# One layer of a hybrid diffusion backbone: where the weights' squares and scales are taken

## The chip, the cores and the metric

The kernel runs on one core of a Trainium2 chip. Time is that of one launch on the device, in microseconds (us), as the median of three runs. Engines are named as the profile names them: PE (TensorE, matmuls; PEld are its weight loads), DVE (VectorE), ACT (ScalarE), POOL (GpSimd) and SP, whose queue issues the DMAs. Every engine runs its own instructions in the order in which they were written into its program.

## The reference, cut to what matters

One layer: RMS norm of tokens with a scale and shift from a conditioning vector, one input projection `w_in`, latent attention beside a pooled branch, gates, an output projection.

```python
mod = jax.nn.silu(c) @ w_mod[l] + b_mod[l]
shift, scale, gate = jnp.split(mod, 3, axis=-1)
h = _rms(x, norm_g[l]) * (1.0 + scale[:, None, :]) + shift[:, None, :]
u = h @ w_in[l]                                   # 2048 tokens, 1024 -> 1984 columns
uc = hc @ w_in[l]                                 # 256 context tokens, own scale and shift
attn = _attend(q, k_all, v_all)                   # q, k, v from columns 0:448 of u
y = _branches(u, attn, w_pool[l], pool_scale[l]) @ w_out[l]
x_new = x + gate[:, None, :] * y
```

Columns 0:448 of `u` feed attention (the "token" columns). Columns 448:1984 are the "features": for each of four groups a pooled input, its gate and the attention gate, 128 columns each, so 12 feature tiles.

## The kernel before, in words

**Precision.** Every product is taken as three matmuls of a high and a low part (hi·hi, hi·lo, lo·hi). In the startup and in block 0 both sides are float32r; from block 1 on they are float16. A float16 weight tile must first be brought to a common range: the sum of its squares is taken, `scl` is its inverse root, the tile is multiplied by `scl` while it is split, and the result is multiplied by `unscl` as it leaves PSUM.

**Stages.** The startup (the list `STARTUP`) loads the modulation weights, makes the scale and shift columns `ac` and `shc`, loads the four token weight tiles (`load_wtok`), and computes the token columns of the first 512 tokens. Then four blocks of 512 tokens run (`feat(b)`, b = 0 to 3), each with 12 feature tiles of two halves of 256 tokens (24 matmuls each half, in `feat_mm`), 96 steps in all. A table `plan` hangs other work on step numbers: token tiles (`tok`, at `TOK_STEPS`), the production of normalised and transposed half blocks hT (`prod`, at `PROD_AT`; the second half of a block is made at the block's start), the float16 token weights (`tok_weights`, at `TW_AT`), the gate row (`gate_row`). From step 88 attention is mixed in, and the output projection ends the kernel. The order in which instructions stand on each engine is made by a scheduler that goes by this program order, by buffers and by its own estimate of times.

**Feature weights.** `load_w(n)` is called from `feat_mm(n - 2)`; tiles 0 to 11 belong to block 0, 12 to 23 to block 1, and from 24 on the finished float16 tiles come back from the DRAM tensor `wd`. In block 0 a loaded tile `raw` is split at once (ACT line 100, DVE line 101). In block 1 `load_w` only loads the same columns again and squares them (line 248, ACT), and `split_w16`, one tile later, goes through a chain: a matmul with ones over one column (`scale_of`, line 227), a sum and a multiply-add on DVE (229, 230), a power on POOL (231), `unscl` on DVE (234, 235), hi on ACT (238), lo on DVE (239), the store to `wd` (257). So the tile for `feat_mm(n)` is split at `feat_mm(n - 1)`.

**Buffers.** `raw` tiles are of tag M (6 buffers), the split tiles, the half blocks and the loaded `x` of tag B (8). PSUM: 5 banks "A", 2 banks "X" (transposes and scale matmuls share them), 1 bank "O". Loads and stores of these stages all go through SP's one queue.

Of the kernel before, what the change touches and what calls it, by code (L numbers as in the profile page):

```python
# [8 lines left out]
F32 = mybir.dt.float32  # L9
F32R = mybir.dt.float32r  # L10
F16 = mybir.dt.float16
AF = mybir.ActivationFunctionType
ALU = mybir.AluOpType
# [3 lines left out]
KT = D // 128  # L17
# [28 lines left out]
X_AT = {0: "c", 11: 2}  # L46
PROD_AT = {"c": (6, 2), 2: (16, 1), 4: (35, 3), 6: (54, 1)}
GATE_AT = (25, 3)
TW_AT = (5, 2)
KV_AT = 79  # L50
Q_AT = 87
ATT_AT = 88
# [15 lines left out]
def tile_hybrid_block(ctx: ExitStack, tc: tile.TileContext, x, c, cx, c_ctx, w_mod, b_mod, norm_g,  # L68
                      w_in, q_lora_g, w_uq, kv_lora_g, w_ukv, q_norm_g, k_norm_g, w_pool,
                      pool_scale, w_out, rope_t, edge_t, out):  # L70
    nc = tc.nc
    x, cx, out = x[0], cx[0], out[0]
# [4 lines left out]
    cst = ctx.enter_context(tc.tile_pool(name="cst", bufs=1))  # L77
# [7 lines left out]
    def nm(s):  # L85
        uid[0] += 1
        return f"{s}{uid[0]}"

    def st(tag, shape, dt=F32):
        return sb.tile([128] + list(shape), dt, tag=tag, bufs=BUFS[tag], name=nm(tag))  # L90

    def pt(tag, shape=(512,), dt=F32):
        return ps.tile([128, *shape], dt, tag=tag, bufs=PBUFS[tag], name=nm("p" + tag))

    def small(n, tag):
        return sm.tile([128, n], F32, tag=tag, name=nm(tag))

    def split(src, hi, lo, eng=None):

        a = nc.scalar.activation(out=hi, in_=src, func=AF.Copy)  # L100
        (eng or nc.vector).tensor_tensor(out=lo, in0=src, in1=hi if hi.dtype == F16 else hi.bitcast(F32),
                                         op=ALU.subtract)
        return a.ins
# [19 lines left out]
    wd = dr.tile([12, 128, 2, KT, 128], F16, name="wd")  # L123
# [6 lines left out]
    nhalf = cst.tile([128, 8], F32, name="nhalf")  # L130
# [4 lines left out]
    ones2 = cst.tile([128, 128], F32, name="ones2")  # L135
# [3 lines left out]
    ssw = cst.tile([128, 20], F32, name="ssw")  # L139
    scl = cst.tile([128, 16], F32, name="scl")  # L140
    unscl = cst.tile([128, 14], F32, name="unscl")
# [9 lines left out]
    def load(out, in_):  # L151

        d = nc.sync.dma_start(out=out, in_=in_)
        if queue:
            if queue[-1] is not None:
                order(queue[-1], d.ins, "order of the first loads")
            queue.append(d.ins)
# [39 lines left out]
    FORDER = [(f, g) for g in range(H) for f in (G_PIN, G_P, G_A)]  # L197
    wq = []

    wraw16 = []  # L200

    def load_w(n):


        if n >= 24:
            w = st("B", [2, KT, 128], F16)
            nc.sync.dma_start(out=w, in_=wd[n % 12])
            wq.append(w)
            return
        f, g = FORDER[n % 12]  # L210
        raw = st("M", [KT, 128])
        load(out=raw, in_=w_in[:, f + g * 128:f + (g + 1) * 128].rearrange("(k p) n -> p k n", p=128))
        if n >= 12:
            square(raw, n % 12)
            wraw16.append((n % 12, raw))
            return
        w = st("B", [2, KT, 128], F32R)
        split(raw, w[:, 0], w[:, 1])
        wq.append(w)


# [2 lines left out]
    def scale_of(c, cols, bound=1.0):  # L224

        p = pt("X")
        nc.tensor.matmul(p[:, 0:cols.stop - cols.start], lhsT=ones2, rhs=ssw[:, cols], start=True, stop=True)
        t = small(1, "sca")
        nc.vector.reduce_sum(t, p[:, 0:cols.stop - cols.start], axis=AX.X)
        nc.vector.tensor_scalar(out=t, in0=t, scalar1=bound * 2.0 ** -30, scalar2=1e-30, op0=ALU.mult, op1=ALU.add)  # L230
        nc.gpsimd.tensor_tensor(out=scl[:, c:c + 1], in0=t, in1=nhalf[:, 0:1], op=ALU.pow)

    def unscale(c, a, b):
        nc.vector.tensor_tensor(out=unscl[:, c:c + 1], in0=scl[:, a:a + 1], in1=scl[:, b:b + 1], op=ALU.mult)
        nc.vector.reciprocal(out=unscl[:, c:c + 1], in_=unscl[:, c:c + 1])

    def split16(src, hi, lo, scale):
        nc.scalar.activation(out=hi, in_=src, func=AF.Copy, scale=scale)  # L238
        nc.vector.scalar_tensor_tensor(out=lo, in0=src, scalar=scale, in1=hi, op0=ALU.mult, op1=ALU.subtract)

    def square(src, c, scale=1.0):
        n = 1
        for k in src.shape[1:]:
            n *= k
        o = junk[:, 0:n]
        if len(src.shape) == 3:
            o = o.rearrange("p (a b) -> p a b", a=src.shape[1])
        nc.scalar.activation(out=o, in_=src, func=AF.Square, scale=scale, accum_out=ssw[:, c:c + 1])

    def split_w16():  # L250

        n, raw = wraw16.pop()
        scale_of(n, slice(n, n + 1))
        unscale(n, n, 13)
        w = st("B", [2, KT, 128], F16)
        split16(raw, w[:, 0], w[:, 1], scl[:, n:n + 1])
        nc.sync.dma_start(out=wd[n], in_=w)
        wq.append(w)

    def mod_scale(si):  # L260
        for i, v in enumerate((ac, shc)):
            square(v[:, :, si], 16 + 2 * si + i, (32.0, 1.0)[i])
        scale_of(13 + si, slice(16 + 2 * si, 18 + 2 * si), 2.0)
        for o, v in ((acs, ac), (shs, shc)):
            nc.vector.tensor_scalar(out=o[:, :, si], in0=v[:, :, si], scalar1=scl[:, 13 + si:14 + si], scalar2=None,
                                    op0=ALU.mult)
# [2 lines left out]

    def tok_weights():  # L270

        scale_of(12, slice(12, 16))
        for si in range(2):
            unscale(12 + si, 12, 13 + si)
        w = st("W", [2, KT, NTOK], F16)
        wt16.append(w)
        for kk in range(4):
            yield
            raw = st("M", [2, NTOK])
            load(out=raw, in_=w_in[kk * 256:(kk + 1) * 256, 0:NTOK].rearrange("(k p) n -> p k n", p=128))  # L280
            k = slice(2 * kk, 2 * kk + 2)
            split16(raw, w[:, 0, k], w[:, 1, k], scl[:, 12:13])

    wth = [st("B", [2304], F32R) for _ in range(2)]
# [6 lines left out]
    def load_wtok(kk):  # L291
        raw = st("M", [2, NTOK])
        load(out=raw, in_=w_in[kk * 256:(kk + 1) * 256, 0:NTOK].rearrange("(k p) n -> p k n", p=128))
        k0 = kk % 2 * 2
        split(raw, wtok[0][kk // 2][:, k0:k0 + 2, :], wtok[1][kk // 2][:, k0:k0 + 2, :],
              nc.gpsimd if kk in WLO_POOL else None)
        square(raw, 12 + kk)

# [373 lines left out]
    nc.vector.memset(gpc, 0.0)  # L674

    def feat_mm(n, halves, got):
        if wraw16:
            split_w16()
        if n + 2 < 48:
            load_w(n + 2)  # L680
        w = wq.pop(0)
        p = pt("A")
        for i, hf in enumerate(halves):
            hi, lo = hT[hf]
            m = 0
            for kt in range(KT):
                for a, b in ((0, hi), (0, lo), (1, hi)):
                    nc.tensor.matmul(p[:, i * HB:(i + 1) * HB], lhsT=w[:, a, kt, :], rhs=b[:, kt, :],  # L688
                                     start=(m == 0), stop=(m == 23))
                    m += 1  # L690
            if i == 0:
                yield
        got.append(p)
# [66 lines left out]
    def gate_row():  # L760
        acc = st("M", [D])
        for k in range(KT):
            yield
            wr = st("M", [D])
            nc.sync.dma_start(out=wr, in_=w_mod[k * 128:(k + 1) * 128, 2 * D:3 * D])
            if k == 0:
                nc.vector.tensor_scalar(out=acc, in0=wr, scalar1=sc[:, 0:1], scalar2=None, op0=ALU.mult)
            else:
                nc.vector.scalar_tensor_tensor(out=acc, in0=wr, scalar=sc[:, k:k + 1], in1=acc,
                                               op0=ALU.mult, op1=ALU.add)  # L770
        yield
        g = st("M", [D])
        bm = st("M", [D])
        nc.sync.dma_start(out=bm[0:1, :], in_=b_mod[2 * D:3 * D].unsqueeze(0))
        for n in range(2):
            p = pt("X")
            nc.tensor.matmul(p[0:1, :], lhsT=ones, rhs=acc[:, n * 512:(n + 1) * 512], start=True, stop=True)
            nc.vector.tensor_tensor(out=g[0:1, n * 512:(n + 1) * 512], in0=p[0:1, :],
                                    in1=bm[0:1, n * 512:(n + 1) * 512], op=ALU.add)
        nc.sync.dma_start(out=gated.unsqueeze(0), in_=g[0:1, :])  # L780

    def iter_call(f, *a):
        f(*a)
        yield
# [7 lines left out]
    plan = {}  # L792
# [6 lines left out]
    for hf, (s0, d) in PROD_AT.items():  # L799
        g = prod(hf)  # L800
        for i in range(4):
            plan.setdefault(s0 + d * i, []).append(g)
    mod_scale(0)
    plan.setdefault(5, []).append(iter_call(mod_scale, 1))
    g = ctx_cols()
    for i in range(5):
        plan.setdefault(i, []).append(g)
    g = tok_weights()
    for i in range(5):
        plan.setdefault(TW_AT[0] + TW_AT[1] * i, []).append(g)  # L810
    g = gate_row()
    for i in range(10):
# [416 lines left out]

    queue.clear()  # L1230
    load_w(1)
    at = attn()
    step = 0
# [109 lines left out]
```

## Time and profile before

| | |
|---|---|
| Time, three runs | median 1253.59 us (1249.56 to 1254.69) |
| Profiled execution, its own time | 1253.44 us |
| Its span, first to last instruction | 1251.6 us |
| Mean granted clock of PE | 0.978 of full |
| DMA | 216.83 MB |

The profiled execution is one more run. Its time beyond the span, 1.84 us, is launch and end. Granted clock 1.0 is 2.4 GHz, 0.5 is 1.2 GHz. The stages stand in the trace like this: the startup until about 60 us, block 0 until 182, block 1 until 310, blocks 2 and 3 with the first scores of attention from there, attention and the output projection from about 450 on.

### The profile page before, as it was taken

The page shows a single profiled execution, that of the slowest core. Times are in us where ns is not written, and L with a number is a line of the kernel's source. Part 1 is how long each engine was busy: PE and PEld are TensorE (multiplying, and loading weights), DVE is VectorE, ACT ScalarE, POOL GpSimd, SP SyncE. Part 2 cuts the span into 40 slices and gives each one's busy share as a digit, 9 for nine tenths or more (in the row PEclk, how much of TensorE's full clock was granted, in tenths as well). Part 3 has the DMA queues.
Part 4 walks back from the last instruction along what each step waited for, and adds up shares of the span by engine and source line. Part 5 has one row for each costly group of instructions (what it writes and reads, how often), then busy time and mean ns, then how long its engine had stood idle before and what let it go on. Part 6 is the DMA issues. An engine that isn't in the chain of part 4 may idle for free.

```text
span 1251.6 us, 22592 instructions
## 1 busy us (share of the span) xinstructions
PE 1178.1 (94%) x7739; PEld 876.3 (70%) x7739; DVE 900.9 (72%) x1749; ACT 767.3 (61%) x1860; POOL 601.2 (48%) x681
## 2 busy tenths in 40 slices
PE   6899988979999999899999999999999999799998
PEld 2699876857778879665666666666666666688887
DVE  4876765565546445469888787878788866999886
ACT  5585676655666455257777777777777766743221
POOL 3655413432435424013656556555655565226666
PEclk9799999979999999999999999999999999999999
DMA  9437755386535556747978788878978788616532
GB/s 305 148 110 183 191 134 180 111 202 201 175 94 140 139 150 147 192 93 161 230 191 197 169 228 193 192 182 205 222 188 190 192 224 193 195 54 207 193 129 99
DMA packets 192586, 216.83 MB, mean 173 GB/s; under 512 B 92707, under 2 KB 145236, under 8 KB 192342
## 3 DMA queue, kind: packets, MB, share of 16 engines
q1 hardware_dynamic: 192470, 215.38, 65.4%
q8 instruction: 61, 1.00, 0.3%
q14 instruction: 55, 0.45, 0.1%
HBM read 100.33 MB, written 41.85 MB: 114 GB/s over the span
## 4 chain that ended last, share of the span: by engine, by line
PE 75%; ACT 6%; DMA 6%; DVE 6%; issue 3%; POOL 2%; SPq 2%; ACTq 0%; DVEq 0%; POOLq 0%
PE pA L882 20%; PE pA L688 17%; PE pA L1156 12%; PE pO L931 6%; PE pA L338 5%; PE pX L931 5%; PE pX L882 2%; PE pA L617 2%; ACT M L964 2%; ACT T L903 2%; DMA M<-in_w_in_dram 1%; SPq L921 1%; DMA B<-in_w_mod_dram 1%; PE pA L592 1%; DMA W<-W 1%
## 5 line engine op out<-in xcount | busy, mean ns | idle before, releaser
L968 POOL TENSOR_TENSOR M<-W,M 128x512 f16<-128x512 f32 x244 | 277.7, 1159 | 254.5 <-ACT M L964 221.0
L882 PE MATMUL pA<-B,M 128*128 128x512 f16 x1280 | 300.6, 380 | 12.3 <-ACT T L903 8.7
L882 PEld LDWEIGHTS <-M 128*128 128x128 f16 x1600 | 156.4, 98 | 153.6 <-issue 14.5
L906 DVE STREAM_TRANSPOSE W<-T 128x512 f32<-128x512 f32 x310 | 192.9, 641 | 72.3 <-ACT T L903 58.2
L964 ACT ACTIVATE M<-W 128x512 f16<-128x512 f32 x279 | 164.6, 632 | 112.6 <-PE pX L931 43.7
L688 PE MATMUL pA<-B,B 128*128 128x256 f16 x1728 | 212.8, 278 | 12.2 <-ACT B L238 4.9
L931 PEld LDWEIGHTS <-B 128*128 128x128 f16 x1728 | 168.5, 98 | 59.1 <-issue 22.3
L688 PEld LDWEIGHTS <-B 128*128 128x128 f16 x1728 | 169.6, 100 | 43.8 <-issue 6.9
L903 ACT ACTIVATE T<-pA,nm,gm 128x512 f32<-128x512 f32 x248 | 188.9, 770 | 16.2 <-DVE nm L891 16.1
L885 DVE TENSOR_REDUCE mx<-pA 128x1 f32<-128x512 f32 x256 | 169.5, 672 | 16.0 <-PE pA L882 15.5
L1156 PE MATMUL pA<-W,M 128*128 128x512 f32 (+1 forms) x528 | 121.0, 388 | 2.3 <-DVE M L1162 2.3
L931 PE MATMUL pO<-M,B 128*128 128x256 f16 x864 | 114.8, 273 | 8.4 <-POOL M L968 3.7
L931 PE MATMUL pX<-M,B 128*128 128x256 f16 x864 | 112.3, 274 | 5.5 <-DVE M L968 2.9
L1156 PEld LDWEIGHTS pA<-W,M 128*128 128x128 f32 x528 | 98.6, 190 | 22.8 <-DVE M L1162 2.7
L688 PE MATMUL pA<-W,B 128*128 128x256 f32 x576 | 78.5, 288 | 0.0
L688 PEld LDWEIGHTS pA<-W,B 128*128 128x128 f32 x576 | 72.8, 192 | 0.3
L1148 POOL TENSOR_TENSOR B<-T,B 128x512 f32<-128x512 f32 x31 | 50.3, 1625 | 29.6 <-DVE T L1183 27.7
L338 PE MATMUL pA<-W,B 128*128 128x448 f16 (+1 forms) x336 | 63.6, 337 | 0.0
L1148 POOL TENSOR_TENSOR T<-T,M 128x512 f32<-128x512 f32 x27 | 43.1, 1596 | 38.4 <-DVE T L1197 27.6
L1161 ACT ACTIVATE M<-B 128x512 fp32r<-128x512 f32 x32 | 19.7, 628 | 51.6 <-PE pA L1156 39.1
L903 ACT ACTIVATION_READ_ACCUMULATOR T<-pA,nm,gm 128x1 f32 x248 | 48.8, 197 | 0.0
L338 PEld LDWEIGHTS <-B 128*128 128x128 f16 x336 | 31.8, 98 | 22.4 <-issue 0.2
(246 smaller groups left out, 1848.2 us busy)
## 6 DMA issues: line engine op xcount, KB each, us to landing
W<-W SPq DMA_DIRECT2D x496, 144.0 KB
M<-in_w_in_dram SPq DMA_DIRECT2D x24, 512.0 KB
B<-wd SPq DMA_DIRECT2D x24, 512.0 KB
B<-in_x_dram SPq DMA_DIRECT2D x16, 512.0 KB
B<-brd SPq DMA_DIRECT2D x8, 1024.0 KB
B<-in_x_dram SPq DMA_DIRECT2D x8, 1024.0 KB
out_dram<-B SPq DMA_DIRECT2D x31, 256.0 KB
wd<-B SPq DMA_DIRECT2D x12, 512.0 KB
```

What stands on the lines that cost most here:

```text
L338: nc.tensor.matmul(p[:, c0:NTOK], lhsT=a[:, kt, k * 128:(k + 1) * 128], rhs=b, start=(kt == 0 and n == 0), stop=(kt == KT - 1 and n == 2))
L617: nc.tensor.matmul(qp[:, 0:384], lhsT=a[:, i, :], rhs=uq[w][:, i, b * 384:(b + 1) * 384], start=(n == 0), stop=(n == 5))
L688: nc.tensor.matmul(p[:, i * HB:(i + 1) * HB], lhsT=w[:, a, kt, :], rhs=b[:, kt, :], start=(m == 0), stop=(m == 23))
L882: nc.tensor.matmul(b[:, s0:s0 + sn], lhsT=q[:, a, c, p % 2, i], rhs=kt[ki][:, kc, o:o + sn], start=(m == 0), stop=(m == 4))
L885: nc.vector.reduce_max(mx[:, n:n + 1], b[:, :w], axis=AX.X)
L903: nc.scalar.activation(out=e[:, :w], in_=sp[n][:, :w], func=AF.Exp, bias=ng, scale=escale, accum_out=rs[:, n:n + 1])
L906: nc.vector.transpose(TP[p][:, :, i, j0:j1, :].rearrange("p q j b -> p j q b"), e[:, :w].rearrange("p (j q b) -> p j q b", q=4, b=32))
L931: i = nc.tensor.matmul(o, lhsT=V[0][:, j, a], rhs=t[:, c, jj], start=(j == 0 and m == 0), stop=(j == NJ - 1 and m == 2))
L964: a = nc.scalar.activation(out=t[:, 0], in_=s2, func=AF.Copy)
L968: lo = eng.tensor_tensor(out=t[:, 1], in0=s2, in1=t[:, 0], op=ALU.subtract)
L1148: eng.tensor_tensor(out=o[:, c0:c1] if op == ALU.mult else xr[:, k, n, c0:c1], in0=o[:, c0:c1], in1=a[:, c0:c1], op=op)
L1156: nc.tensor.matmul(b[:, c0:c1], lhsT=c[:, x0, kt, :], rhs=w[x1][:, kt, c0:c1], start=(first and kt == kts[0] and m == 0), stop=(last_ and ...
```

## The change

The squares of the feature tiles move from block 1 to block 0, where each tile is loaded for the first time; `feature_scales` makes all twelve scales at once, at `feat_mm(10)`. In block 1 `load_w(n)` then splits the tile where it loads it, one tile earlier in the program than before. The squares of the token weights leave the startup: `tok_weights` takes them from the hi halves `wth` at step 3 (with a bound of 2 in the scale) and goes on at steps 5 to 13, as before. `mod_scale(0)` moves from ahead of step 0 to step 2.

```diff
-TW_AT = (5, 2)
+TW_AT = (3, 2)
     def load_w(n):
         if n >= 12:
-            square(raw, n % 12)
-            wraw16.append((n % 12, raw))
-            return
-        w = st("B", [2, KT, 128], F32R)
-        split(raw, w[:, 0], w[:, 1])
+            w = st("B", [2, KT, 128], F16)
+            split16(raw, w[:, 0], w[:, 1], scl[:, n - 12:n - 11])
+            nc.sync.dma_start(out=wd[n - 12], in_=w)
+        else:
+            w = st("B", [2, KT, 128], F32R)
+            split(raw, w[:, 0], w[:, 1])
+            square(raw, n)
         wq.append(w)
-    def split_w16():
-
-        n, raw = wraw16.pop()
-        scale_of(n, slice(n, n + 1))
-        unscale(n, n, 13)
-        w = st("B", [2, KT, 128], F16)
-        split16(raw, w[:, 0], w[:, 1], scl[:, n:n + 1])
-        nc.sync.dma_start(out=wd[n], in_=w)
-        wq.append(w)
+    def feature_scales():
+
+        p = pt("X")
+        nc.tensor.matmul(p[:, 0:12], lhsT=ones2, rhs=ssw[:, 0:12], start=True, stop=True)
+        t = cst.tile([128, 12], F32, name="fsc")
+        nc.vector.tensor_scalar(out=t, in0=p[:, 0:12], scalar1=2.0 ** -30, scalar2=1e-30, op0=ALU.mult, op1=ALU.add)
+        nc.gpsimd.tensor_tensor(out=scl[:, 0:12], in0=t, in1=nhalf[:, 0:1].broadcast_to([128, 12]), op=ALU.pow)
+        nc.vector.tensor_scalar(out=unscl[:, 0:12], in0=scl[:, 0:12], scalar1=scl[:, 13:14], scalar2=None, op0=ALU.mult)
+        nc.vector.reciprocal(out=unscl[:, 0:12], in_=unscl[:, 0:12])
     def tok_weights():
-        scale_of(12, slice(12, 16))
+        for i in range(4):
+            square(wth[i // 2][:, i % 2 * 896:i % 2 * 896 + 896].bitcast(F32), 12 + i)
+        yield
+        scale_of(12, slice(12, 16), 2.0)
     def load_wtok(kk):
-        square(raw, 12 + kk)
     def feat_mm(n, halves, got):
-        if wraw16:
-            split_w16()
+        if n == 10:
+            feature_scales()
-    mod_scale(0)
+    plan.setdefault(2, []).append(iter_call(mod_scale, 0))
     g = tok_weights()
-    for i in range(5):
+    for i in range(6):
```

Lines of the changed kernel below are a few higher for the same code (548 was 546, 327 was 325, 559 was 557, 646 was 644).

ACT at the start of block 0, before: T are token results leaving PSUM (line 546) and being squared (557), B_630, B_637 and B_792 are the feature tiles 1 to 3, M their raw tiles.

```order
L100 ACTIVATE W_115<-T_529 128x512
L546 COPY T_610<-pA_240 128x448
L100 ACTIVATE B_630<-M_628 128x1024
L557 ACTIVATE junk,us_669<-T_610 128x256
L557 ACTIVATE junk,us_669<-T_610 128x128
L546 COPY T_612<-pA_247 128x448
L557 ACTIVATE junk,us_669<-T_610 128x64
L100 ACTIVATE B_637<-M_635 128x1024
L100 ACTIVATE B_792<-M_790 128x1024
```

The same place after the change (B_617, B_625 and B_781 are tiles 1 to 3).

```order
L100 ACTIVATE W_115<-T_526 128x512
L100 ACTIVATE B_617<-M_615 128x1024
L248 ACTIVATE junk,ssw<-M_615 128x1024
L100 ACTIVATE B_625<-M_623 128x1024
L248 ACTIVATE junk,ssw<-M_623 128x1024
L548 COPY T_607<-pA_239 128x448
L100 ACTIVATE B_781<-M_779 128x1024
L548 COPY T_609<-pA_246 128x448
L559 ACTIVATE junk,us_658<-T_607 128x256
L559 ACTIVATE junk,us_658<-T_607 128x128
L559 ACTIVATE junk,us_658<-T_607 128x64
```

The first token result now stands behind two splits and two squares; before it stood ahead of all of them.

ACT at the change from block 0 to block 1, before: B_2154 is the float16 feature tile 12, the first of block 1; pX_2101 and pA_2190 belong to token tiles, pA_2161 is the result of feature tile 11.

```order
L738 ACTIVATE T_2065<-pA_2070 128x512
L100 ACTIVATE B_1856<-T_2060 128x512
L642 ACTIVATE T_2106<-pX_2101,gqk 128x512
L599 ACTIVATE junk,sk_2194<-pA_2190 128x128
L586 ACTIVATE T_2186<-T_1968 128x128
L599 ACTIVATE junk,sk_2194<-pA_2190 128x128 x3
L238 ACTIVATE B_2154<-M_2067,scl 128x1024
L744 ACTIVATE T_2235<-pA_2161 128x512
```

The same place after (B_2088 is tile 12, B_2170 tile 13).

```order
L327 ACTIVATE T_2072<-pX_2067,shs,acs 128x256 x2
L238 ACTIVATE B_2088<-M_2086,scl 128x1024
L100 ACTIVATE T_2119<-pX_2117 128x128
L740 ACTIVATE T_2077<-pA_2092 128x512
L238 ACTIVATE B_2170<-M_2168,scl 128x1024
L100 ACTIVATE B_1867<-T_2072 128x512
L644 ACTIVATE T_2128<-pX_2123,gqk 128x512
```

Tile 12 moved ahead of the token tile's work and of the gate's result, and tile 13, which before came some ten rows later, now stands close behind it.

SP's queue at the same place, before: B_2245 is the half block of `x` that `prod(3)` turns into hT for the second half of block 1; kd and vd are stores of keys and values; M_2546 is the raw tile 16.

```order
L153 DMA M_2546<-in_w_in_dram 128x8x128
L589 DMA vd<-T_1980 128x256
L644 DMA kd<-T_2106 128x4x128
L652 DMA kd<-U_2117 128x4x128
L645 DMA kd<-T_2107 128x4x128
L589 DMA vd<-T_2186 128x256
L153 DMA B_2245<-in_x_dram 128x1024 x2
L745 DMA gad<-T_2235 128x512
L756 DMA brd<-T_2242 128x504
L257 DMA wd<-B_2154 128x2048
```

And after (B_2258 is that half block of `x`, B_2088 and B_2170 the tiles 12 and 13, M_2529 the raw tile 16).

```order
L591 DMA vd<-T_1992 128x256
L153 DMA M_2529<-in_w_in_dram 128x8x128
L153 DMA B_2258<-in_x_dram 128x1024 x2
L214 DMA wd<-B_2088 128x2048
L767 DMA M_2560<-in_w_mod_dram 128x1024
L646 DMA kd<-T_2128 128x4x128
L214 DMA wd<-B_2170 128x2048
L647 DMA kd<-T_2129 128x4x128
L591 DMA vd<-T_2199 128x256
```

The load of `x` moved ahead of the three stores of keys that stood before it. In both programs SP has 465 rows; no DMA is added or removed.

## Rows read from the trace of the kernel before

**Rows 1.** The page, part 1: busy time of each engine, its share of the span, instructions.
```profile
...
PE 1178.1 (94%) x7739; PEld 876.3 (70%) x7739; DVE 900.9 (72%) x1749; ACT 767.3 (61%) x1860; POOL 601.2 (48%) x681
...
```

**Rows 2.** Windows: length, busy time and count by engine, granted clock, DMA.
```profile
...
60.00:182.00 122.00, 116.88 (x891) 112.06 (x890) 84.09 (x186) 82.74 (x232) 52.44 (x88) 0.97 0.59 152
182.00:310.00 128.00, 110.31 (x807) 87.19 (x808) 75.38 (x168) 76.70 (x188) 43.94 (x84) 0.92 0.60 172
310.00:450.00 140.00, 139.59 (x1070) 112.80 (x1068) 72.67 (x155) 83.88 (x256) 57.38 (x116) 1.00 0.54 142
450.00:1252.00 802.00, 767.33 (x4816) 538.44 (x4814) 628.41 (x1172) 488.66 (x1126) 415.04 (x365) 0.99 0.69 178
...
```

**Rows 3.** PE's waits, 182 to 310: in total, times, longest.
```profile
...
PE pA L688 <- ACT B L238: 4.9, 3, 3.2
PE pA L688 <- DVE B L239: 4.7, 2, 2.3
PE pX L227 <- DVE U L651: 2.1, 2, 1.8
PE pX L657 <- DVE U L651: 2.1, 1, 2.1
PE pA L688 <- DVE B L101: 1.4, 3, 0.5
PE pX L320 <- ACT T L325: 1.0, 2, 0.8
...
```

**Rows 4.** Timeline of PE: start, duration, instruction, idle before it and what ended it.
```profile
...
58.50 1.11 PE L338 MATMUL pA<-B,W 128*128 128x448 f32 x2 [1.26 <-DVE W L101]
...
188.36 4.87 PE L688 MATMUL pA<-B,B 128*128 128x256 f16 x22 [2.32 <-DVE B L239]
...
223.06 0.28 PE L227 MATMUL pX<-ssw,ones 128*128 128x1 f32 x2
223.20 2.78 PE L688 MATMUL pA<-B,B 128*128 128x256 f16 x24
...
261.78 4.36 PE L688 MATMUL pA<-B,B 128*128 128x256 f16 x24
...
276.03 5.30 PE L688 MATMUL pA<-B,B 128*128 128x256 f16 x24 [2.34 <-DVE B L239]
...
```

**Rows 5.** Timeline of ACT, at four places.
```profile
...
69.96 0.54 ACT L546 COPY T<-pA 128x448 f32<-128x448 f32 x1 [1.36 <-PE pA L338]
...
72.87 1.05 ACT L100 ACTIVATE B<-M 128x1024 fp32r<-128x1024 f32 x1
...
122.96 1.06 ACT L100 ACTIVATE B<-M 128x1024 fp32r<-128x1024 f32 x1 [2.44 <-DMA M<-in_w_in_dram]
...
184.45 1.15 ACT L238 ACTIVATE B<-M,scl 128x1024 f16<-128x1024 f32 x1 [0.97 <-POOL scl L231]
...
```

**Rows 6.** Line 239, VectorE's half of the split: shortest, median, longest ns.
```profile
...
L239 DVE SCALAR_TENSOR_TENSOR B<-M,scl,B x12: 1256/1278/1286, 187.0 to 306.3; 128x1024 f16<-128x1024 f32 x12
...
```

**Rows 7.** Line 111, powers on POOL, one column and four.
```profile
...
L111 POOL TENSOR_TENSOR kvr<-kvm,nhalf x18: 542/576/911, 73.7 to 471.5; 128x1 f32<-128x1 f32 x18
L111 POOL TENSOR_TENSOR kr<-km,nhalf x18: 1012/1018/1029, 85.9 to 489.1; 128x4 f32<-128x4 f32 x18
...
```

**Rows 8.** Timeline of SP's queue around the load of the fourth half block.
```profile
...
181.63 0.37 SPq L644 DMA_DIRECT2D kd<-T  x1
...
184.16 0.87 SPq L153 DMA_DIRECT2D B<-in_x_dram  x2
...
```

**Rows 9.** Line 248, the squares: one instruction and its read of the sum.
```profile
...
L248 ACT ACTIVATE junk<-M x16: 933/1056/1098, 15.3 to 289.1; 128x1024 bf16<-128x1024 f32 x12, 128x896 bf16<-128x896 f32 x4
L248 ACT ACTIVATION_READ_ACCUMULATOR junk<-M x16: 185/187/243, 16.1 to 290.1; 128x1 f32 x16
...
```

**Rows 10.** PE's waits, 60 to 182.
```profile
...
PE pO L751 <- ACT T L100: 3.2, 1, 3.2
PE pA L592 <- ACT T L100: 1.5, 1, 1.5
```

More of the change, by code (lines that the diff above doesn't have):

```diff
@@ L198, in tile_hybrid_block @@
     wq = []
-    wraw16 = []
     def load_w(n):
```

## Prediction

> **What bounds the kernel now.** I read the page's first part, then the windows by stage, then PE's waits in the stages where PE is not full, and last the timelines around those waits. PE is busy 94% of the span, and no other engine comes near it [rows 1], so time is won where PE stands idle or runs at the half clock, and lost where the change makes it stand. The windows say where that is [rows 2]: block 0 (60 to 182) has 122.00 - 116.88 = 5.1 us without PE work, block 1 (182 to 310) has 128.00 - 110.31 = 17.7 us and a mean granted clock of 0.92, and from 310 to 450 PE is busy 139.59 of 140.00 us at clock 1.00. What block 1 is shortened by is therefore not taken back by a wait in the stage behind it, as far as the order of the instructions there stays the same, which it does past block 2 but for a few swaps of neighbours.
>
> What PE waits for in block 1 [rows 3]: 4.9 us for line 238 and 4.7 us for line 239, the two halves of the split that close the chain of a feature tile, and 2.1 us at line 227, the chain's own matmul, which waits for a bank "X" that a token tile still holds (`U` of line 651). Another 2.1 us go to a transpose waiting for the same tile, 1.4 and 1.0 us to the hT of the next half block. ACT's row at 184.45 shows the chain from its other side: the split has waited 0.97 us for the power of line 231 [rows 5].
>
> The clock: 24 matmuls of a half take 2.78 us at full clock. After 2.32 us of idle time 22 of them take 4.87, after 2.34 us 24 take 5.30, and between them stands one half of 4.36 [rows 4]; these are the rows that answer to a granted clock of 1.2 GHz in place of 2.4. Against the undisturbed half that is 4.87 - 22/24 x 2.78 = 2.3, 5.30 - 2.78 = 2.5 and 4.36 - 2.78 = 1.6, in all 6.4 us.
>
> **The change, part by part.** The sum is made against the profiled execution's 1253.4 us, which stands 0.15 us below the median of the three runs.
>
> *The chain leaves block 1.* Twelve chains go, and the tile is split one tile earlier, a time in which PE has about 2 x 2.78 = 5.6 us of matmuls to do. The split itself needs 1.15 on ACT and 1.28 on DVE, one after the other, 2.4 us [rows 5, 6], so it fits under one tile unless the raw tile or a buffer is late. I take all of 4.9 + 4.7 + 2.1 = 11.7 us as gone. Three things come in their place. First, one chain remains, at the border of the blocks: matmul, DVE, POOL, ACT, DVE. The power over 12 columns has no row; one column takes 0.55, four take 1.02 [rows 7], and a line through both gives 0.39 + 12 x 0.157 = 2.3 us; the bounds are 1.0 (no more than four columns) and 12 x 0.55 = 6.6. I take 2.3, since two rows give it. With the split's 2.4 the chain is 4.7 and some 0.5 for the small operation on DVE. PE has behind the chain's matmul 16 matmuls of tile 11 (16 x 0.116 = 1.9 us) and some small token work of about as many columns as 12 such matmuls (an estimate, 1.4 us): 3.3 us. That leaves 1.9. Second, ACT now has tile 13's split ahead of the copy that finishes the hT of the first half of block 1; I count 0.4 for that, bounded by zero and the split's 1.15. Third, the bank "X" for which line 227 waited is still wanted by the next transpose: 1.0 of the 2.1 us stays. Against that stands the load of `x` for the second half of block 1. In before it was issued at 184.16, behind a store of keys issued at 181.63 [rows 8]; it now stands ahead of the stores, and of the 2.4 us of hT waits (1.4 + 1.0, [rows 3]) I take 1.0 as won. Net: -11.7 + 1.9 + 0.4 + 1.0 - 1.0 = -9.4 us. Bounds: nothing left of any wait in the block, -17.7; or the power at 6.6 and both `X` waits whole, -4.
>
> *The clock in block 1.* With the two longest gaps gone their halves run at full clock. One gap of about 2.3 us is left at the border, so I take back 5.0 of the 6.4 us (bounds 2.3, if each border wait again costs a half, and 6.4).
>
> *The matmuls of the chain.* 15 scale matmuls become 4, eleven fewer, each 0.14 us from its start to the start of the next [rows 4]: -1.5 us, since PE is what the stage runs on.
>
> *The startup.* Four squares of about 1.0 us leave ACT [rows 9]. The last wait of PE there is on DVE (line 101, 1.26 us, [rows 4]), whose work for the tiles stays, so most of this is hidden: -0.5, between 0 and -1.3. The modulation columns' squares only move to step 2, where nobody waits for them for the next steps: 0.
>
> *Block 0 pays.* ACT gets 12 squares of feature tiles (1.06 and 0.19 for the read of the sum, [rows 9]) and 4 of token weights; two of the twelve lay in this window before. That is 10 x 1.25 + 4 x 1.05 = 16.7 us, and ACT goes from 82.74 to 99.4 of 122 us, 81%, below PE's 116.88 [rows 2]. On average it is not the bound; the cost is in order. At the start the first token result, which left PSUM at 69.96, stands after the change behind two splits and two squares, the first of which began at 72.87 [rows 5]: its turn comes at about 72.87 + 1.05 + 1.25 = 75.2, 5.2 us later. In PE's order about one half of a feature tile is put ahead of the work that needs it, some 2.6 us, so 2.6 are uncovered. Later in the block a square can stand ahead of a result for which PE waits; I put 1.4 on that, a bit more than one square. Total +4. Bounds: nothing (the squares run in ACT's gaps), or all of the 16.7 and more.
>
> Here a row speaks against the change. At 122.96 ACT's split waited 2.44 us for a raw tile [rows 5], and in the same block PE waited 3.2 us at line 751 and 1.5 at line 592 for ACT's line 100 [rows 10]: whatever ACT is made to hold, what stands behind it is held as well. The Trainium skill, "Perfetto Trace Analysis", section "Tensor Engine Instruction (MATMUL, LD_WEIGHTS)", says that ACT, DVE and GPSIMD take their work strictly first in, first out, and only PE can reorder a little. The trace agrees, with those 2.44 and 3.2 us. By that rule each of the twelve squares is a delay of 1.25 us for all results behind it on ACT, and if PE waited for each of them, the time would be the one of the third rival below.
>
> **Sum.** -9.4 - 5.0 - 1.5 - 0.5 + 4.0 = -12.4, and 1253.4 - 12.4 = 1241.0 us.
>
> **The rivals.**
>
> *The wait only changes its name.* The splits of block 1 come earlier by a tile, but so must the raw tiles; if the load, a buffer of tag M or B, or a bank "X" is what comes last next, half of the 11.7 us stays and with it half of the clock: -12.4 + 5.9 + 2.5 = -4.0, or 1249; with a little luck at the buffers 1246. For it speaks that the 2.1 us at line 657 are already such a wait [rows 3]; against it, that the longest waits name lines 238 and 239 and not a DMA.
>
> *Block 0 eats the gain.* ACT at 81% delays results often enough that block 0 becomes 12 us longer instead of 4: 1249; at 16 us longer, 1253. For it speaks the stall of [rows 10], against it ACT's free 22.6 us.
>
> *Slower.* The place is ACT in block 0, by its order: each of the sixteen squares stands ahead of a result that PE or a PSUM bank needs at once, and PE's waits grow by the squares' 16.7 us and the 2.6 of the first result, plus a clock that falls after each larger gap as in [rows 4], two or three times 2.4 us. That is 19.3 + 6 = 25 in place of 4, so 1262. It decides from a block 0 that is 23 us longer (6.3 us above no change). Against it: ACT's work had 39 us of free time there, and raw tiles come early enough that squares can fall into it.
>
> **How the numbers follow.** A measurement of this kernel tells about 0.5% (6.3 us) from no change. My forecast has 0.68; the first rival 0.14, on the border of the 0.5%, so half of it counts as faster; the second 0.10, most of it within 0.5%; the third 0.08. Faster: 0.68 x 0.95 + 0.07 + 0.02 = 0.74; within 0.5%: 0.17; slower: 0.09. The range: down to 1229 the sum takes the larger bounds of the waits in block 1 (-17.7 in place of -9.4, whole clock) and block 0 free or nearly so; up to 1251 it holds the first rival and the lighter half of the second.
>
> **What would show it.** Right: in block 1 PE's waits for the split's two lines are nearly gone, the granted clock is about 1.0 there, block 1 is 14 to 18 us shorter and block 0 about 4 us longer, with a new or longer wait of PE at its start for the copies of the token results (now behind squares on ACT). Wrong: waits of the same size in block 1 under another name (raw tiles by DMA, `U` of the token tile); waits for ACT spread over all of block 0, with ACT busy 95% there; a chain at the border that is longer than 5 us, with the power over 12 columns well over 2.3; or a startup that moves by more than 1.3 us in either direction.

## The result, and the profile of the changed kernel

The changed kernel takes 1239.57 us in the median of four runs (1236.57 to 1241.11); the kernel before took 1254.14 beside it. The ratio is 0.9888, with a 95% interval of 0.9858 to 0.9919: 1.1% faster, where 1241 was forecast. The profiled execution is the quickest of the four, 1236.57 us with a span of 1234.8, so its differences to the trace of before are a little larger than those of the medians (16.8 us of span against 14.6).

The page's first part, which answers to [rows 1]: PE is 8.9 us less busy, and since the span is 16.8 shorter, 7.9 us less idle.

```profile
...
PE 1169.2 (95%) x7717; PEld 871.5 (71%) x7717; DVE 894.6 (72%) x1704; ACT 765.8 (62%) x1860; POOL 597.3 (48%) x670
...
```

To place the difference, the stages need ends that are nearly the same work in both programs. Two events on ACT serve for that: the result of feature tile 9 leaving PSUM, near the end of block 0, and that of tile 21, near the end of block 1 (line 708 before, 710 after). Of the kernel before, from the timeline of ACT:

```profile
...
168.30 0.63 ACT L708 ACTIVATE T<-pA 128x512 f32<-128x512 f32 x1
...
302.93 0.69 ACT L708 ACTIVATE T<-pA,unscl 128x512 f32<-128x512 f32 x1 [0.92 <-PE pA L688]
```

And of the changed kernel:

```profile
...
174.68 0.63 ACT L710 ACTIVATE T<-pA 128x512 f32<-128x512 f32 x1
...
287.83 0.69 ACT L710 ACTIVATE T<-pA,unscl 128x512 f32<-128x512 f32 x1 [0.60 <-PE pA L690]
```

Tile 9 is 6.4 us later, tile 21 is 15.1 us earlier. Between the two lie 134.63 us before and 113.15 after. The cut at tile 9 is exact to about 1 us only: of block 0's tile matmuls 89 stand behind it before and 81 after, and 8 of them are about 1.1 us of PE's time (16 take 2.16 below). The windows with these ends (columns as in [rows 2]), before:

```profile
...
60.00:168.30 108.30, 103.41 (x786) 99.62 (x786) 75.23 (x167) 72.54 (x205) 49.88 (x83) 0.97 0.65 166
168.30:302.93 134.63, 116.71 (x850) 93.23 (x849) 78.62 (x175) 83.95 (x213) 45.03 (x87) 0.92 0.56 157
...
```

After, and behind it the stretch that follows up to 460 us:

```profile
...
60.00:174.68 114.68, 106.34 (x799) 102.37 (x798) 73.83 (x172) 87.38 (x235) 45.19 (x83) 0.95 0.62 157
174.68:287.83 113.15, 107.24 (x822) 86.29 (x821) 75.97 (x134) 70.88 (x191) 45.02 (x75) 0.98 0.67 191
287.83:460.00 172.17, 171.76 (x1325) 138.95 (x1323) 88.43 (x191) 101.41 (x317) 69.17 (x139) 1.00 0.53 141
...
```

In the stretch of block 1, idle time of PE falls from 134.63 - 116.71 = 17.9 us to 113.15 - 107.24 = 5.9, and its busy time by 9.5, with the granted clock going from 0.92 to 0.98. In block 0 idle time grows from 4.9 to 8.3 and busy time from 103.41 to 106.34, at a clock of 0.95 in place of 0.97. Behind tile 21 PE is full, 171.76 of 172.17 us, so what block 1 gained is kept. From tile 21 to the end of the span it is 948.7 us before and 947.0 after; that last 1.7 us is less than two profiles of the changed kernel differ by in this stretch (below), so no part of the change is read from it.

PE's waits between 182 and 310, which answer to [rows 3]:

```profile
...
PE pA L690 <- DVE B L239: 1.1, 2, 0.9
PE pX L322 <- ACT T L327: 1.0, 2, 0.8
PE pA L690 <- ACT B L238: 0.6, 1, 0.6
PE pX L659 <- DVE U L653: 0.5, 1, 0.5
PE pX L659 <- DVE T L645: 0.4, 1, 0.4
PE pA L690 <- DVE B L101: 0.3, 1, 0.3
...
```

The 9.6 us for the two lines of the split have become 1.7, the wait at line 227 is gone with the line, and what line 657 waited for (now 659) is 0.9 in place of 2.1. Of the hT waits the 1.4 us fell to 0.3, and the 1.0 stayed to the tenth.

The border of the blocks, first on PE, then the power on POOL, then ACT:

```profile
...
182.71 0.28 PE L253 MATMUL pX<-ssw,ones 128*128 128x12 f32 x2
182.84 2.16 PE L690 MATMUL pA<-W,B 128*128 128x256 f32 x16
...
188.11 0.39 PE L690 MATMUL pA<-B,B 128*128 128x256 f16 x2
188.69 1.92 PE L690 MATMUL pA<-B,B 128*128 128x256 f16 x16 [0.19 <-DVE B L239]
...
```

```profile
...
183.28 2.64 POOL L256 TENSOR_TENSOR scl<-fsc,nhalf 128x12 f32<-128x12 f32 x1 [4.24 <-DVE fsc L255]
...
```

```profile
...
186.17 1.15 ACT L238 ACTIVATE B<-M,scl 128x1024 f16<-128x1024 f32 x1
...
187.84 1.16 ACT L238 ACTIVATE B<-M,scl 128x1024 f16<-128x1024 f32 x1
188.88 0.64 ACT L100 ACTIVATE B<-T 128x512 f16<-128x512 f32 x1
...
```

From the chain's matmul at 182.71 the power is done at 185.9, ACT's half of tile 12 at 187.3, and PE starts tile 12 at 188.11 with small work in between; it waits 0.19 us for DVE's half. Tile 13's split stands ahead of the copy that completes hT (188.88), but PE's next wait behind 188.69 comes at 200.6, so nobody is held up by that. The chain takes 6.0 us from its matmul to the end of DVE's half (182.71 to about 188.7), more than the 5.2 of the prediction. PE has other work for nearly all of it: its gaps from 182.84 to 188.69 add up to 1.0 us, and of these only the 0.19 names the split. So the border chain, which looked like 1.9 us, is nearly free.

Block 0 pays. ACT is late in the place that was named, but PE does not stand there. ACT, where the first token results leave PSUM:

```profile
...
72.63 1.06 ACT L100 ACTIVATE B<-M 128x1024 fp32r<-128x1024 f32 x1 [1.23 <-DMA M<-in_w_in_dram]
73.59 1.04 ACT L248 ACTIVATE junk<-M 128x1024 bf16<-128x1024 f32 x1
...
74.63 0.51 ACT L548 COPY T<-pA 128x448 f32<-128x448 f32 x1
...
```

The first token result begins at 74.63, behind the second of two splits and squares, where it began at 69.96 before [rows 5]: 4.7 us later. PE does not stop for it: from 60 to 82 us it is busy 22.00 of 22.00 us in both kernels, since matmuls of feature tiles stand in between. It begins to lose time behind that. The window from 82 to 112 us, before and after:

```profile
...
82.00:112.00 30.00, 29.88 (x229) 28.82 (x228) 18.91 (x47) 19.02 (x69) 17.89 (x35) 1.00 0.41 94
...
```

```profile
...
82.00:112.00 30.00, 27.38 (x207) 26.01 (x206) 18.83 (x53) 23.50 (x79) 14.99 (x29) 1.00 0.35 82
...
```

PE's waits from 60 to 182, which answer to [rows 10]:

```profile
...
PE pO L753 <- ACT T L100: 4.2, 1, 4.2
PE pA L594 <- ACT T L100: 3.1, 3, 1.5
PE pX L581 <- DVE T L101: 1.0, 1, 1.0
```

The stall of line 751 (now 753) has grown from 3.2 us to 4.2, and the 1.5 of line 592 (now 594) is there as before. New are 1.6 us more for line 594, at 89 and 110 us, and the 1.0 of line 581, at 108: three short waits for a split of token work, where there was none. ACT shows what stands ahead of the copy that line 753 waits for:

```profile
...
121.47 1.06 ACT L248 ACTIVATE junk<-M 128x1024 bf16<-128x1024 f32 x1 [2.29 <-DMA M<-in_w_in_dram]
...
124.49 1.06 ACT L248 ACTIVATE junk<-M 128x1024 bf16<-128x1024 f32 x1 [0.79 <-DMA M<-in_w_in_dram]
...
126.45 1.97 ACT L238 ACTIVATE W<-M,scl 128x896 f16<-128x896 f32 x2
...
128.83 2.00 ACT L100 ACTIVATE B<-M 128x1024 fp32r<-128x1024 f32 x2
130.72 0.62 ACT L100 ACTIVATE T<-T 128x504 fp32r<-128x504 f32 x1
...
```

Two squares wait 2.29 and 0.79 us for raw tiles, and behind them stand two splits of token weights, two splits of feature tiles, and then, at 130.72, the result for PE. Before, one split waited 2.44 us at that place [rows 5].

### The profile page after: what moved, and what is told of

It reads as the page before. It is cut to its first block, busy times and chain, and to the rows that moved or that the text cites. A ratio compares the mean times of both kernels' runs of the same rounds, so it can differ in the third digit from the quotient of the medians.

```text
span 1234.8 us, 22505 instructions
## 1 busy us (share of the span) xinstructions
PE 1169.2 (95%) x7717; PEld 871.5 (71%) x7717; DVE 894.6 (72%) x1704; ACT 765.8 (62%) x1860; POOL 597.3 (48%) x670
## 4 chain that ended last, share of the span: by engine, by line
PE 71%; DMA 7%; ACT 7%; DVE 6%; SPq 4%; issue 2%; POOL 1%; ACTq 0%; DVEq 0%; POOLq 0%
PE pA L884 19%; PE pA L690 15%; PE pA L1158 13%; PE pO L933 5%; PE pA L340 5%; PE pX L933 5%; SPq L923 3%; PE pX L884 2%; PE pA L619 2%; ACT M L966 2%; ACT T L905 1%; DMA M<-in_w_in_dram 1%; DVE T L371 1%; DMA W<-W 1%; DMA W<-in_w_mod_dram 1%
## 5 line engine op out<-in xcount | busy, mean ns | idle before, releaser
L690 PE MATMUL pA<-B,B 128*128 128x256 f16 x1728 | 207.0, 274 | 2.4 <-DVE B L239 1.1
```

## The experiments

Times of single profiled executions differ by some us behind tile 21, where all these kernels are alike: from there to the end of the span it is 948.7 us in before, 947.0 in the changed kernel and 951.6 in a second profile of it, 941.9 to 951.6 in the experiments. The event of tile 9 differs less between two profiles of one kernel: 174.68 and 175.05 us in the changed kernel, 169.84 and 171.12 in the one with quarter squares. So the mechanisms are read from the events of tiles 9 and 21, and the totals from the medians with their intervals.

### The features' part alone

Against the changed kernel (dots stand for lines left out):

```diff
-TW_AT = (3, 2)
+TW_AT = (5, 2)
...
     def tok_weights():
-        for i in range(4):
-            square(wth[i // 2][:, i % 2 * 896:i % 2 * 896 + 896].bitcast(F32), 12 + i)
-        yield
-        scale_of(12, slice(12, 16), 2.0)
+        scale_of(12, slice(12, 16))
...
     def load_wtok(kk):
...
+        square(raw, 12 + kk)
...
-    plan.setdefault(2, []).append(iter_call(mod_scale, 0))
+    mod_scale(0)
...
-    for i in range(6):
+    for i in range(5):
```

> The kernel before with the features' part of the change alone: feature squares in block 0, one chain for twelve scales, split one tile earlier; token squares stay in the startup and mod_scale(0) ahead of step 0. If the gain is block 1's alone: 1240 us, within 3 of the whole change, with block 1's waits gone and block 0 about 6 us longer. If the token part carries part of the gain or of block 0's loss: 4 us or more away from the whole change, and block 0 longer by clearly less than 6 us.

1239.73 us, ratio 0.9869 (0.9853 to 0.9885). Tile 9 at 174.21, block 1 up to tile 21 113.16 us: the whole change without its token part gives the same events, to half a microsecond. This is the first expectation: the gain and most of the loss are the features'.

### The token part alone

The diff is the other half of the change's, put on the kernel before: `TW_AT`, the squares in `tok_weights`, `mod_scale(0)` at step 2.

> The kernel before with the token part of the change alone: squares of token weights and mod_scale some steps later. If the features' part does everything: 1252 to 1254 us, block 1 as before with about 9 us of waits of PE for lines 238 and 239. If the four squares in the startup were on the path, 3 us or more faster; if their new place in block 0 delays token results, 3 us or more slower.

1250.23 us, ratio 0.9967 (0.9948 to 0.9987), 0.3% faster. The 4.4 us against the kernel before beside it (1254.59) are the number of the second expectation, but not its reason, a shorter startup. The trace does not show where they are won: block 1 is as before, with 5.8 and 4.6 us of PE's waits for lines 239 and 238, and tile 9 is 2.8 us later, not earlier.

```profile
...
60.00:171.08 111.08, 105.07 (x787) 101.16 (x786) 75.34 (x169) 76.13 (x212) 46.34 (x82) 0.95 0.63 162
171.08:304.52 133.44, 114.64 (x854) 92.47 (x853) 78.83 (x175) 83.89 (x214) 44.68 (x87) 0.92 0.56 159
...
```

Up to tile 21 this profile is 1.6 us behind that of before; the 6.8 us that it wins lie behind, in work that the edit does not touch. No theory of it is taken as shown.

### The chain one tile earlier

```diff
     def load_w(n):
...
             square(raw, n % 12)
             wraw16.append((n % 12, raw))
+            split_w16()
             return
...
     def feat_mm(n, halves, got):
-        if wraw16:
-            split_w16()
```

This stands on the kernel with the token part alone.

> The token part plus one edit of block 1: square, chain and split of a tile all stand where the tile is loaded, one tile earlier than before; the chain still runs for each tile, and block 0 has no feature squares. If what counted was that the split stands one tile earlier: block 1's waits are gone and, since block 0 keeps its length, the time is 1234 to 1239 us, below the whole change. If what counted is the chain itself (square 1.25, matmul, DVE, power 0.55, then 2.4 of split, with ACT held in between): half of the 9.6 us of waits and of the slow clock stays, 1244 to 1250 us.

1254.24 us, ratio 0.9988 (0.9971 to 1.0005): nothing won, and both expectations missed. Block 1 is no shorter than before:

```profile
...
169.65:305.76 136.11, 118.89 (x855) 93.58 (x854) 80.47 (x179) 83.93 (x215) 44.40 (x86) 0.91 0.54 156
...
```

PE's waits between 180 and 310 (line numbers are one higher here), and under them ACT's for the power:

```profile
...
PE pA L689 <- ACT B L239: 4.3, 4, 2.7
PE pX L660 <- DVE T L646: 4.3, 1, 4.3
PE pX L642 <- ACT T L328: 3.0, 2, 2.6
...
```

```profile
...
ACT junk L249 <- DMA M<-in_w_in_dram: 7.7, 4, 3.0
ACT B L239 <- POOL scl L232: 6.6, 4, 2.4
...
```

Before, the same view of ACT (182 to 300 in both) had these rows:

```profile
...
ACT junk L248 <- DMA M<-in_w_in_dram: 9.0, 4, 4.2
...
ACT B L238 <- POOL scl L231: 3.3, 3, 1.4
...
```

With square, chain and split close together in the program, ACT stands at the split and waits for POOL, 6.6 us in place of 3.3, and what stands behind it on ACT is held as well; of PE's waits 4.3 and 3.0 us are now for token work and hT. Ahead of each chain ACT also stands at the square until the raw tile has landed, 7.7 us here and 9.0 before. The changed kernel has no squares in this stage; its splits wait 3.9 us for raw tiles.

### Scales ready, split one tile later

```diff
     def load_w(n):
         if n >= 12:
-            w = st("B", [2, KT, 128], F16)
-            split16(raw, w[:, 0], w[:, 1], scl[:, n - 12:n - 11])
-            nc.sync.dma_start(out=wd[n - 12], in_=w)
...
+            late.append((n, raw))
+            return
+    def split_late():
+        n, raw = late.pop()
+        w = st("B", [2, KT, 128], F16)
+        split16(raw, w[:, 0], w[:, 1], scl[:, n - 12:n - 11])
+        nc.sync.dma_start(out=wd[n - 12], in_=w)
+        wq.append(w)
     def feat_mm(n, halves, got):
         if n == 10:
             feature_scales()
+        if late:
+            split_late()
```

> The whole change, but the split of a tile in block 1 stands one tile later, where it stood before; the scales are ready from the one chain. If the chain was what counted: the split's 2.4 us fit under the 5.6 us of one tile, the waits stay gone, 1240 us, within 3 of the whole change. If it was the earlier place: PE waits for lines 238 and 239 come back with 4 us or more and the clock falls again, 1246 us or more.

1248.12 us, ratio 0.9940 (0.9920 to 0.9959): under half of the gain, the number of the second expectation. The window of block 1:

```profile
...
173.46:297.05 123.59, 111.51 (x822) 89.39 (x821) 76.01 (x135) 71.39 (x191) 41.81 (x76) 0.93 0.63 175
...
```

Idle time is 12.1 us and the clock 0.93. PE's waits (lines are six to eight higher in this kernel: 698 is the feature matmuls, 244 and 245 the split):

```profile
...
PE pX L328 <- DVE B L194: 3.5, 2, 2.8
PE pX L665 <- DVE T L651: 3.4, 1, 3.4
PE pX L672 <- DVE T L101: 1.7, 1, 1.7
PE pA L698 <- DVE B L245: 1.2, 1, 1.2
...
PE pA L698 <- ACT B L244: 0.4, 1, 0.4
...
```

The split's own lines cost 1.6 us, as little as in the whole change: there the first expectation is right. But 8.6 us of waits for DVE have come up in the token work and in the making of hT; 3.4 of them stand at line 665, the transpose at which the whole change waits 0.9 (its line 659). For these the trace shows what stood ahead. DVE's row of line 651 begins at 264.30, right behind a row that had waited for a store of keys:

```profile
...
263.96 0.43 DVE L611 TENSOR_TENSOR U<-kr,kr 128x256 f32<-128x256 f32 x1 [2.71 <-DMA kd<-U]
...
```

So with the later split a wait comes back there under another name. For the other 5.2 us the cause stays open: with the split, the scheduler moved other rows too. The two halves of block 1's edit thus work together. Against the 133.44 us of the token part alone, scales ready and split late give 123.59, chain and split early give 136.11, and both together 113.15. "Scales ready" is itself several things at once: the squares with their waits for raw tiles, the chain's rows on PE and DVE, and the power all leave block 1. No run takes these apart.

### The squares in block 0: none, a quarter, whole, double

```diff
-            square(raw, n)
```

with `nc.vector.memset(ssw[:, 0:12], 1.0)` at the start, then

```diff
-            square(raw, n)
+            square(raw[:, 0:2], n)
...
-scalar1=2.0 ** -30
+scalar1=4 * 2.0 ** -30
```

and last `square(raw, n)` written twice. All three are edits of the changed kernel.

> The whole change without the twelve feature squares: their sums are a constant, so this part of the computation is left out; the one chain, the early splits and the token part stay. If the squares on ACT are what makes block 0 longer: the result of tile 9 leaves PSUM at 169.5 to 171.5 us (before 168.3, changed kernel 174.7), and the time is 1234 to 1237 us. If block 0 is longer for other reasons (the token part, the order of the rest, buffers): tile 9 stays at 173 us or later and the time within 2 us of the changed kernel.

> The whole change with each feature square taken over two of eight row groups and the sum multiplied by four: the scale is then an estimate of the range and no bound on it. A square is 0.45 us on ACT in place of 1.25. If the squares' time on ACT sets block 0's loss: tile 9 at 171 to 173 us, time between that without squares and the changed kernel, 1236 to 1238 us, so faster than both kernels. If it is their places in the order and not their length: no change from the changed kernel within 2 us.

> The whole change with every feature square done twice in block 0 (15 us more on ACT). If the loss follows ACT's time as the twelve squares have it (some 3.6 us for 15 us): tile 9 at 177 to 179 us and 1242 to 1245 us. If ACT then has no gaps left to take them: tile 9 at 183 us or later and 1248 us or more. If squares are hidden: within 2 us of the changed kernel.

| squares | tile 9 at | tile 9 to 21 | median | ratio (95%) |
|---|---|---|---|---|
| none | 170.36 | 113.11 | 1237.82 | 0.9857 (0.9831 to 0.9883) |
| a quarter | 169.84 | 113.04 | 1233.90 | 0.9829 (0.9802 to 0.9855) |
| whole | 174.68 | 113.15 | 1239.57 | 0.9888 (0.9858 to 0.9919) |
| double | 178.14 | 114.42 | 1243.43 | 0.9904 (0.9881 to 0.9927) |

The row of whole squares is the first measurement of the changed kernel; the others were taken on one chip, so the ratios compare better than the medians. The windows up to tile 9, without squares, with a quarter, and double, and for the first and last the stretch of block 1 (ACT's busy time is the number ahead of the fourth bracket):

```profile
...
60.00:170.36 110.36, 104.52 (x784) 100.16 (x783) 75.45 (x169) 76.05 (x211) 47.07 (x82) 0.95 0.63 163
170.36:283.47 113.11, 108.48 (x836) 88.22 (x836) 75.25 (x134) 70.61 (x191) 42.90 (x74) 0.98 0.67 191
...
```

```profile
...
60.00:169.84 109.84, 104.21 (x788) 99.99 (x787) 74.64 (x169) 80.42 (x233) 47.42 (x82) 0.96 0.63 163
...
```

```profile
...
60.00:178.14 118.14, 107.74 (x805) 102.17 (x804) 74.98 (x169) 99.35 (x257) 46.72 (x83) 0.95 0.60 152
178.14:292.56 114.42, 108.00 (x816) 86.27 (x815) 75.15 (x134) 70.86 (x190) 44.96 (x76) 0.97 0.67 190
...
```

Whole squares cost 174.68 - 170.36 = 4.3 us at tile 9, the second helping 3.5: against 11.3 and 12.0 us by which ACT's busy time up to there grows (76.05, 87.38, 99.35), about a third of it. Part of this is order only: without squares 92 tile matmuls of block 0 stand behind tile 9's result, with whole squares 81, with double ones 75. At tile 21, where that no longer counts, the prices are 4.4 and 4.7 us (283.47, 287.83 and 292.56), about 0.4 of ACT's added time. Block 1's length moves by 0.0 and 1.3 us, so the price arises in block 0 for the most part. Quarter squares add nothing at tile 9 that can be told from none.

Without squares tile 9 came out as the first expectation had it, and the time 0.8 us above it; with double squares both did. Quarter squares came out faster than either expectation, at tile 9 and in time. The medians follow the squares less well: without any, the kernel takes 3.9 us more than with quarter squares, though its tile 21 is only 0.6 later, and the intervals of none, whole and double overlap. So the price rests on the events of tiles 9 and 21, each from a single execution.

### Quarter squares once more, beside the changed kernel

Three kernels on one chip: quarter squares on the features' part alone, the changed kernel again, and quarter squares on the whole change again.

> The features' part alone (token squares in the startup, mod_scale(0) ahead of step 0) with quarter squares: sum over two of eight row groups times four, an estimate of the range and no bound. If the token part only moves work: within 2 us of quarter squares on the whole change, 1232 to 1236 us, tile 9 at 169 to 171. If the token part is needed for the gain of the quarter squares: 1238 us or more and tile 9 at 173 or later.

> The changed kernel once more, on the chip and beside the runs of the two kernels with quarter squares. If squares cost what the experiments with none, full and double gave (some 4 us at tile 9): 4 to 6 us slower than the whole change with quarter squares, 1238 to 1241 us. If the difference was one of the runs: within 2 us of it.

> The whole change with quarter squares once more, on the same chip: 1232 to 1236 us, below the changed kernel by 4 to 6 us, if the price of the squares on ACT is real; 1237 us or more if the first measurement was a lucky one.

1236.78 us (0.9858, 0.9839 to 0.9878), 1241.01 us (0.9890, 0.9872 to 0.9907) and 1233.83 us (0.9838, 0.9817 to 0.9858). Tile 9 at 172.77, 175.05 and 171.12. Quarter squares on the whole change are the quickest version of this study, 7.2 us under the changed kernel on the same chip, where 4 to 6 was expected; of the 7.3 us between the spans of the two profiles 3.9 lie ahead of tile 9, 0.3 in block 1 and 3.1 behind tile 21, and these last are not explained. On the features' part alone they fell between the two expectations, tile 9 a little later than thought and 3.0 us slower in the median. The version gives up a guarantee: the sum of all squares bounds the largest entry, a quarter of them only estimates it.

## Why the prediction was right, and where its sizes were off

**The sum.** Forecast -12.4 us to 1241.0, measured -14.6 in the medians, -16.8 in the profiles, which divide into +6.4 up to tile 9, -21.5 in block 1 and -1.7 behind it. The sign and the mechanism in block 1 were right; the sizes were not. Block 1 gave 5.6 us more than its terms (-9.4 - 5.0 - 1.5 = -15.9), and the stages ahead of it took 2.9 more than theirs (+4.0 - 0.5 = +3.5). That these errors have opposite signs, so that the medians came within 2.2 us of the forecast, is luck. Of the signs of being right, the waits for the split nearly went and block 0 became longer; PE's new wait at the start of block 0 did not come, and block 1 became shorter than the 14 to 18 us. Of the signs of being wrong, the border chain of more than 5 us came, at almost no cost.

**The chain leaves block 1: -9.4 forecast, -12.0 of idle time measured.** The waits for the split went as forecast: 9.6 us became 1.7. Of these 0.19 stand at the border, where the prediction kept 1.9, and 1.5 at one later tile, at 268 and 269 us. The border chain was longer than summed, 6.0 us in place of 5.2, with the power over 12 columns at 2.64 us, more than the 2.3 of the line through two rows; but PE had some 4.9 us of work behind the chain's matmul, not the 3.3 that were counted. The largest error is the bank "X": lines 227 and 657 had 4.2 us of waits between them, the prediction left 3.1 of them (the 2.1 of line 657 untouched and 1.0 of line 227's), and 0.9 were left, at line 659. The hT waits lost 1.1 (0.6 forecast, 1.0 won less 0.4 for tile 13's split), but these were waits for DVE; the 1.0 for ACT stayed, although the load of `x` was issued at 176.33 in place of 184.16, so that the earlier load won them is not shown. The prediction's ground for the whole term, that the split fits under one tile once the chain is gone, held only in part: it took ready scales and the earlier place for one thing, and the experiments show that the earlier place without ready scales gives nothing, and ready scales without it about half of block 1's gain.

**The clock and the scale matmuls: -5.0 and -1.5 forecast, -9.5 of busy time measured.** An estimate of the clock's part: in windows of 2 us, PE's busy time times what the granted clock lacks to 1.00 adds up to 8.3 us before (168 to 304) and to 1.3 after (174 to 288), so 7.0 of the 9.5 us are the clock. About 1.1 are the eight tile matmuls that now stand ahead of tile 9, and the rest is near the 1.5 for the scale matmuls. The prediction's 6.4 us for the whole loss came from three halves in [rows 4]. The granted clock was low only there, from about 187 to 194, 258 to 266 and 275 to 282 us, but PE had transposes and token work at the lower clock too, which the halves leave out. After the change one such stretch is left, from 268 to 272, behind a wait of 0.93 us, and none at the border, where the prediction kept one.

**The startup: -0.5 forecast, nothing won.** Tile 0's result left PSUM at 77.15 before and at 78.11, 77.20 and 77.21 in three kernels with the token part and without squares in block 0. The token squares had been hidden, as the bound of 0 had it. PE waits for DVE there in any case: 2.0 us at line 402 before, 3.8 at the same line, now 404, after. In the changed kernel the result came at 79.25, later and not earlier.

**Block 0: +4.0 forecast, +6.4 measured.** 4.3 of it are the feature squares, by the runs with none. That is near the term, and the first token result was 4.7 us later (5.2 forecast), but the step from there to the time was wrong: the 2.6 us that were to be uncovered at that result did not appear, with PE full until 82 us. PE's waits came later in the block, where the prediction had put 1.4 us: three new ones of 2.6 us together, and 1.1 more at line 753. Without squares two of the three are there as well, at 0.4 and 0.6 us. The other 2.1 us at tile 9 came with the rest, the order of which the token part changes; the features' part alone loses 5.9 there with the startup as before, so the parts do not add up, and how these 2.1 us divide stays open.

**The rivals.** The wait that only changes its name came up in both experiments that made half of block 1's edit, with token work and hT as the new names; in the late split 3.4 us of it came from a store of keys that a buffer waited for. Block 0 eats 6.4 us of what block 1 gives, under a third of it. The slower end, every square uncovered, is far off: even doubled squares put tile 9 only 9.8 us behind before, where 23 were needed. The rule of the Trainium skill, "Perfetto Trace Analysis", section "Tensor Engine Instruction (MATMUL, LD_WEIGHTS)", that ACT works strictly first in, first out, agrees with what ACT shows at 121.47 and with its 6.6 us behind POOL's power in the early chain. The price here was 4.4 us at tile 21 for 11.3 us more of work on ACT, far from a delay of PE by every square.

## What to carry to other kernels

Work that is put on an engine with free time can cost a part of its length, where it stands ahead of something that the bound engine needs; here about 0.4 of it, measured by leaving it out and doubling it. That a result comes later on its engine is not yet a loss: the first token result came 4.7 us later, and PE had other work until then. A chain over several engines that ends in a wait at the head of an in-order engine holds up what stands behind it; here it helped to make it once, ahead of its use, and it did not help to start it earlier at the same place. And where a stage runs at a lower mean clock, all the work in its slow stretches belongs in the sum, not only the rows in which it is seen best.

## What the runs showed of the hardware that was not expected

- The power on POOL over 12 columns took 2.64 us, and 2.64 or 2.65 in every other run that has it; one column takes 0.54 to 0.58 and four 1.02 [rows 7]. From four to twelve that is 0.20 us a column, where from one to four it was 0.15 to 0.16.
- The stages behind tile 21, with nearly the same work in all kernels, took between 941.9 and 951.6 us from profile to profile, and 947.0 and 951.6 in two profiles of one kernel: more than most terms of the sum.
